# Decoder layer on one core: gate blocks fetched while the last gate blocks are made, and one DRAM tile for each projection and gate block

## The chip, the cores and the metric

The kernel runs on one core of one Trainium2 chip. The metric is the device time of one execution in microseconds, lower is better. Five engines work side by side, each through its own list of instructions in order: TensorE (PE, with PEld for its weight loads), VectorE (DVE), ScalarE (ACT), GpSimd (POOL) and SyncE (SP). In this kernel SP issues the DMAs. An engine waits for another only through semaphores.

## The reference

One layer of a hybrid decoder on 1024 prompt tokens and 32 sample tokens that share their weights, all in fp32:

```python
h = layer_norm(ALPHA * x + 0.5 * swiglu(x, f1_w1, f1_w3, f1_w2), ln1_g, ln1_b)
z = h @ w_in + b_in
...
att = combine_groups(outs, lses).astype(h.dtype)
yb, vrows = sgu_branch(uv, sgu_ln_g, sgu_ln_b, sgu_ws, sgu_b)
mix = (jax.nn.sigmoid(ga) * (att @ w_oa) + jax.nn.sigmoid(gb) * (yb @ w_ob)) @ w_out
h = layer_norm(ALPHA * h + mix, ln2_g, ln2_b)
h = layer_norm(ALPHA * h + 0.5 * swiglu(h, f2_w1, f2_w3, f2_w2), ln3_g, ln3_b)
```

`z` has 5,376 columns: queries, keys and values of three attention groups, the two halves of the gated MLP (SGU), and the gates `ga` and `gb`, 1024 columns each. `combine_groups` weighs the three attention groups by a softmax over their log-sums. `att` has 256 columns, `yb` 512, the model 1024.

## The kernel before, in words

All activations are kept transposed, features on the 128 partitions and the 1056 tokens along the free axis, cut into NC = 4 chunks of C = 264. Every fp32 operand of a large matmul is split into a high and a low part (`split`, L238 on ScalarE and L239 on VectorE), and `mm3` (L227) makes each 128-row product of three matmuls. The 42 column blocks of `z` (128 columns each) are numbered: 0–17 are q, k, v; 18–25 the SGU; 26–33 the blocks of `ga`; 34–41 those of `gb`.

The Tile framework takes the program in the order in which the code names it, sorts each engine's list by a priority that follows that order, and adds the waits. `high_priority(offset=URGENT)` moves what is under it ahead of what the code named shortly before. Tiles come from pools that turn round: 37 slots (`S`, 4.1 KB a partition each), 8 weight tiles (`W`), 2 raw weight tiles (`R`), 6 mid tiles (`M`), 3 PSUM banks for products (`mm_tile`) and 5 for all else (`ax_tile`). An allocation waits until the last user of the tile that it takes over is done. DMAs all go through SP's list, one behind the other, so one that must wait holds all behind it.

**widen** computes `z`. Its first six gate blocks (34 to 39, already with their sigmoid) and all q, k, v and SGU blocks are written to the DRAM scratch `zD`, by `gate8` (L939) and `send` (L1020). `fetch_z` (L1084) brings a whole block of 128 x 1056 back into a slot, with the DMA of L1086.

**mix** makes the last ten gate blocks: six one after the other, then the last four chunk by chunk (the loop over `c` that ends in L1514), each by `gate8`: 24 matmuls into a product bank, a bias on ScalarE into a mid tile (L938), a store to `zD` (L939). `tick` runs, between such steps, pieces of three queues of generators: attention blocks (`attend`, which ends in the store of its statistics L1213), the SGU and `combine` (`mid`), and the sample tokens' attention (`sample`, `sample_join`, L1340 to L1382).

Then follows w_ob. `local(n)` (L1491) is the block n of `yb @ w_ob`: 12 matmuls for each chunk into a product bank, then the product multiply L1489, on VectorE, which multiplies the fetched gate block `mt[n]` (block 34 + n) in place. The first EARLY = 6 run by themselves; then for each n the w_oa product of the same form on `ta[n]` (block 26 + n, 6 matmuls a chunk), with `local(6)` and `local(7)` ahead of n = 0 and 1. Gate blocks made in mix (LATE_GATES: 40, 41 and 26 to 33) get their sigmoid after the fetch, on ScalarE. `mt[n] += ta[n]` (L1564) and a split give the operand of w_out.

Beside the first of these `local` blocks runs `combine(1)`: it loads the attention's minima and sums from DRAM (`mlD`, L1231 to L1237), computes the three groups' weights on 16 partitions (L1245 to L1258), stores them (`cD`, L1260), loads them back spread over 64 partitions each (L1267, six loads of 256 KB), and multiplies and adds the three groups (L1272, L1274, L1275 on 128 x 1024). Its result is split by `split_att` for w_oa. `column_sums` (L1524, L1526) loads blocks of w_out and reduces them in the same stretch.

Of the kernel before, what the change touches and what calls it, by code (L numbers as in the profile page):

```python
# [12 lines left out]
F32 = mybir.dt.float32  # L13
# [7 lines left out]
P = 128  # L21
D = 1024
KB = D // P
NP = 1024
NS = 32
NT = NP + NS
# [28 lines left out]
URGENT = 300  # L55
# [24 lines left out]
class Trunk:  # L80
# [950 lines left out]
    def widen(self):  # L1031
        nc, a = self.nc, self.a
        self.att = [None, None]
        self.attT = {}
        self.mlD = self.dp.tile([2, 3, 2, 2, NP], F32, name="mlD")
        self.cD = self.dp.tile([2, 3, 2, NP], F32, name="cD")
        self.sD = self.dp.tile([3, 3, 4, NS, 64], F32, name="sD")
        self.jD = self.dp.tile([6, 64, 66], F32, name="jD")
        self.zD = self.dp.tile([42, P, NT], F32, name="zD")
        lns, self.lns = self.lns, {}  # L1040
        self.A, Y = self.normed, self.Y
        self.Y = None
        self.T, self.L = ({}, {}), {}
        units, self.early = self.early, None
        preps = {}

        def begin(f):
            preps[f] = self.prep(a["wz7"][f], f, KH * P, nc.gpsimd if f else nc.vector)
            next(preps[f])

        self.drain(lns[NC - 2])
        self.step(self.bg, 1)
        self.slow.append(self.spread(0, Y, self.A, nc.vector))
        for c in range(NC):
            self.drain(lns.pop(c))
            if c == NC - 1:
                self.slow.append(self.spread(1, Y, self.A, nc.vector))
            for n in range(CHUNKED):
                self.gate8(units[n], DENSE[n], c, AF.Sigmoid, STEPS["lead"], 1)
        units = Y = None  # L1060
        for n in range(CHUNKED, NLEAD):
            w = self.unit(a["wzp"][n])
            if n == NLEAD - 1:
                begin(0)
            for c in (1, 3, 0, 2):
                self.gate8(w, DENSE[n], c, AF.Sigmoid, STEPS["lead"], 1)
                if n == NLEAD - 1:
                    next(preps[0], None)
        self.A = None
        for f in range(NZ):  # L1070
            for _ in preps.pop(f):
                pass
            if f < NZ - 1:
                begin(f + 1)

            def between():
                if f + 1 in preps:
                    next(preps[f + 1], None)
                self.tick(STEPS["strassen"], 1)

            self.pair(f, between)
            del self.L[f]
# [389 lines left out]
    def mix(self):  # L1472
        nc, a = self.nc, self.a
        att, mt = [], [None] * KB
# [8 lines left out]
        def product(wo, xs, c, t):  # L1483
            p = self.mm_tile()[:, :C]
            cc = slice(c * C, c * C + C)
            for k, (xh, xl) in enumerate(xs):
                self.mm3(p, wo, k * P, xh[:, cc], xl[:, cc], k == 0, k == len(xs) - 1)
            with self.urgent():
                nc.vector.tensor_tensor(t[:, cc], t[:, cc], p, op=ALU.mult)  # L1489

        def local(n):  # L1491
            wb = self.unit(a["wo"][n, :, 2 * P :], 4 * P)
            if n + 2 < KB:
                mt[n + 2] = self.fetch_z(36 + n)
            if 34 + n in LATE_GATES:
                nc.scalar.activation(mt[n], mt[n], AF.Sigmoid)
            for c in range(NC):
                product(wb, self.yb, c, mt[n])
                self.tick(STEPS["wob"], 1)
# [10 lines left out]
                self.gate8(w, DENSE[n], c, AF.Identity, STEPS["tail"], 1)  # L1510
        units = {n: self.unit(a["wzp"][n]) for n in range(NLEAD + NTAIL - LAST, NLEAD + NTAIL)}
        for c in range(NC):
            for n in units:
                self.gate8(units[n], DENSE[n], c, AF.Identity, STEPS["tail"], 1)  # L1514
        units = self.A = None
        for n in range(2):
            mt[n] = self.fetch_z(34 + n)
        while any(g in self.mid for g in sgu):
            self.step(self.mid, 1)
        def column_sums():  # L1520
# [24 lines left out]
        for n in range(EARLY):  # L1545
            local(n)
# [6 lines left out]
        for n in range(KB):  # L1553
            wa = self.unit(a["wo"][n], 2 * P)
            if n + 2 < KB:
                ta.append(self.fetch_z(28 + n))
            if n < KB - EARLY:
                local(EARLY + n)
            if 26 + n in LATE_GATES:
                nc.scalar.activation(ta[n], ta[n], AF.Sigmoid)  # L1560
            for c in range(NC):
                product(wa, att, c, ta[n])
                self.tick(0, 1)
            nc.vector.tensor_tensor(mt[n], mt[n], ta[n], op=ALU.add)  # L1564
            m2.append((self.S([P, NT], F32R), self.S([P, NT], F32R)))
            self.split(*m2[n], mt[n])
            done += 1
# [204 lines left out]
```

## Time and profile before

| | |
|---|---|
| median of 3 runs | 2226.13 us (2225.06 to 2228.02) |
| the profiled run | 2225.12 us, of which the span that the profile covers is 2223.3 us |
| mean granted TensorE clock | 0.986 |
| busy share of TensorE, VectorE, ScalarE, GpSimd | 97%, 70%, 40%, 15% |
| last store of the last gate blocks | issued 1302.4 us into the span |
| products of w_ob and w_oa | about 1301 to 1406 us into the span |

The profile is one execution, its times are counted from the start of the span. "Busy" is the time in which an engine executes an instruction; "idle before" is what it waited ahead of one, with the instruction that ended the wait (`<-DVE S L1489`: a VectorE instruction of line 1489 that wrote or freed an S tile). In the windows, the granted clock is a share of TensorE's full speed, and the DMA share the mean busy share of the core's 16 DMA engines. The names of tiles stand without their numbers.

### The profile page before, as it was taken

To read this page: it belongs to the slowest core of one execution; us is meant where nothing else is said; L and a number is where in the kernel's file an instruction comes from. 1 tells how busy PE (TensorE), PEld (TensorE's weight loads), DVE (VectorE), ACT (ScalarE), POOL (GpSimd) and SP (SyncE) were. 2 spreads that over 40 slices of the span, in tenths; PEclk is the share of its full clock that TensorE was granted. 3 is DMA by queue.
4 is the path that set the end of the run, shared out by engine and by line. 5 is a ranking of instruction groups with operands and counts; after the bars stand their busy time and mean duration, and the time that the engine had idled before them with its cause. 6 is when DMAs were issued, how large, how long until landed. Compare 5 with 4: busy or idle time off the path is not lost. (4 is left out here: it accounts for less than half of the span.)

```text
span 2223.3 us, 43147 instructions
## 1 busy us (share of the span) xinstructions
PE 2148.0 (97%) x17281; PEld 2095.8 (94%) x17281; DVE 1560.7 (70%) x2698; ACT 898.6 (40%) x1684; POOL 327.1 (15%) x238
## 2 busy tenths in 40 slices
PE   9999999999999999999989969998999999999997
PEld 8999999999999999999879759898999999999997
DVE  8776677656689537787475546778767676657787
ACT  5444444321126533435464533246444444421124
POOL 0433333100000112231000000000422332200000
PEclk9999999999999999999999989999999999999998
DMA  4445445697953336667745455513444545595831
GB/s 156 144 141 186 167 156 184 196 368 266 354 198 131 109 122 208 210 216 247 257 154 174 127 162 193 212 54 116 168 159 165 185 157 179 196 362 218 309 117 79
DMA packets 163640, 416.83 MB, mean 187 GB/s; under 512 B 24096, under 2 KB 60688, under 8 KB 160752
## 3 DMA queue, kind: packets, MB, share of 16 engines
q1 hardware_dynamic: 163008, 413.55, 53.4%
q8 instruction: 135, 2.21, 0.4%
q14 instruction: 65, 0.53, 0.1%
q10 hardware_dynamic: 432, 0.54, 0.1%
HBM read 301.64 MB, written 158.57 MB: 207 GB/s over the span
## 5 line engine op out<-in xcount | busy, mean ns | idle before, releaser
L227 PE MATMUL mm<-S,W 128*128 128x264 f32 x5040 | 677.4, 289 | 43.3 <-DVE S L1489 27.9
L227 PE MATMUL ax<-S,W 128*128 128x264 f32 x5472 | 716.6, 284 | 0.6 <-ACT S L978 0.5
L227 PEld LDWEIGHTS mm<-S,W 128*128 128x128 f32 x5040 | 640.5, 191 | 59.7 <-DVE S L1489 28.1
L227 PEld LDWEIGHTS ax<-S,W 128*128 128x128 f32 x5472 | 685.7, 188 | 3.2 <-ACT S L978 1.9
L227 PE MATMUL ax<-S,S 128*128 128x264 f32 x3288 | 484.7, 284 | 2.2 <-DVE S L987 2.2
L227 PEld LDWEIGHTS ax<-S,S 128*128 128x128 f32 x3288 | 434.5, 188 | 4.3 <-DVE S L987 3.3
L227 PE MATMUL mm<-S,S 128*128 128x264 f32 x2496 | 389.1, 286 | 7.1 <-ACT S L238 4.0
L227 PEld LDWEIGHTS mm<-S,S 128*128 128x128 f32 x2496 | 338.2, 189 | 8.9 <-ACT S L238 4.2
L238 ACT CAST W<-R 128x256 fp32r<-128x256 f32 (+2 forms) x172 | 127.9, 760 | 367.0 <-PE ax L227 134.3
L369 POOL TENSOR_TENSOR Q<-R 128x512 f32<-128x512 f32 x50 | 70.2, 1403 | 792.5 <-DMA R<-w13b 215.9
L239 DVE TENSOR_TENSOR W<-R,W 128x256 fp32r<-128x256 f32 (+2 forms) x172 | 148.4, 870 | 30.4 <-ACT W L238 30.1
L238 ACT CAST W<-Q 128x1024 fp32r<-128x1024 f32 (+1 forms) x79 | 77.8, 984 | 194.9 <-POOL Q L370 90.6
L444 DVE TENSOR_TENSOR S<-ax,M 128x264 f32<-128x264 f32 x84 | 33.4, 433 | 151.7 <-PE ax L227 151.7
L781 DVE SCALAR_TENSOR_TENSOR S<-ax,S 128x264 f32<-128x264 f32 x240 | 99.1, 428 | 56.7 <-PE ax L227 56.2
L239 DVE TENSOR_TENSOR S<-Q,S 128x1024 fp32r<-128x1024 f32 (+2 forms) x87 | 125.7, 1445 | 6.5 <-ACT S L238 5.6
L106 POOL CAST S<-ones 128x1 fp32r<-128x1 f32 x32 | 15.7, 506 | 773.4 <-DVE S L1564 385.4
L238 ACT CAST S<-Q 128x1024 fp32r<-128x1024 f32 (+2 forms) x87 | 86.3, 992 | 100.6 <-PE ax L227 71.7
L239 DVE TENSOR_TENSOR W<-Q,W 128x1024 fp32r<-128x1024 f32 (+1 forms) x79 | 92.3, 1169 | 24.5 <-ACT W L238 24.5
L239 DVE TENSOR_TENSOR S<-S,M 128x528 fp32r<-128x528 f32 x72 | 84.7, 1176 | 3.0 <-ACT M L238 1.3
L370 POOL TENSOR_TENSOR Q<-Q,R 128x512 f32<-128x512 f32 x50 | 84.8, 1696 | 2.7
L238 ACT CAST S<-R 128x512 fp32r<-128x512 f32 (+1 forms) x65 | 44.4, 686 | 94.9 <-DMA sumsA<-S 43.5
L377 POOL TENSOR_TENSOR Q<-R,Q 128x512 f32<-128x512 f32 x50 | 82.2, 1645 | 1.2
(201 smaller groups left out, 2069.6 us busy)
## 6 DMA issues: line engine op xcount, KB each, us to landing
ws<-st SPq DMA_DIRECT2D x144, 256.0 KB
S<-sumsA SPq DMA_DIRECT2D x63, 528.0 KB
S<-sumsB SPq DMA_DIRECT2D x63, 528.0 KB
M<-kv SPq DMA_DIRECT2D x96, 256.0 KB
sumsA<-M SPq DMA_DIRECT2D x90, 264.0 KB
sumsB<-M SPq DMA_DIRECT2D x90, 264.0 KB
R<-w13b SPq DMA_DIRECT2D x44, 512.0 KB
S<-zD SPq DMA_DIRECT2D x42, 528.0 KB
```

What stands on the lines that cost most here:

```text
L106: self.nc.gpsimd.tensor_copy(t[:, 0, :1] if len(shape) == 3 else t[:, :1], self.ones[:, :1])
L227: mm = lambda a, b, s, e: nc.tensor.matmul(o, a[:, cc], b, start=s, stop=e, skip_group_check=True)
L238: a = self.nc.scalar.copy(hi, src)
L239: b = self.nc.vector.tensor_tensor(lo, src, hi.bitcast(F32), op=ALU.subtract)
L369: tt(s12[:, lo], cd[:, lo], cd[:, hi], op=ALU.add)
L370: tt(s12[:, hi], s12[:, lo], ab[:, lo], op=ALU.subtract)
L377: tt(s34[:, hi], ab[:, hi], s12[:, hi], op=ALU.subtract)
L444: go(one, 5, False, lambda x: tt(h[:, x, 1], one[x], p7[:, x], op=ALU.add))
L781: nc.vector.scalar_tensor_tensor(y(x, r, e), bank[x], HALF, y(x, r, e), op0=ALU.mult, op1=ALU.add)
```

## The change

The scratch `zD` becomes a list of 42 DRAM tiles, one a block, where it was one tile. The fetches of blocks 34 to 39 move from behind the gate loops (two) and from `local(0)` to `local(3)` (four) into the loop of the last gate blocks: two each ahead of chunks 1, 2 and 3, under high priority. `local(0)` and `local(1)` now fetch blocks 40 and 41, under high priority too. Lines from 1494 on move down, by one behind the fetch of `local`, by three behind the gate loop.

```diff
--- before.py
+++ after.py
@@ -1036,7 +1036,7 @@
         self.cD = self.dp.tile([2, 3, 2, NP], F32, name="cD")
         self.sD = self.dp.tile([3, 3, 4, NS, 64], F32, name="sD")
         self.jD = self.dp.tile([6, 64, 66], F32, name="jD")
-        self.zD = self.dp.tile([42, P, NT], F32, name="zD")
+        self.zD = [self.dp.tile([P, NT], F32, name=f"zD{n}") for n in range(42)]
         lns, self.lns = self.lns, {}
         self.A, Y = self.normed, self.Y
         self.Y = None
@@ -1490,8 +1490,9 @@
 
         def local(n):
             wb = self.unit(a["wo"][n, :, 2 * P :], 4 * P)
-            if n + 2 < KB:
-                mt[n + 2] = self.fetch_z(36 + n)
+            if n + 6 < KB:
+                with self.tc.high_priority(offset=URGENT):
+                    mt[n + 6] = self.fetch_z(40 + n)
             if 34 + n in LATE_GATES:
                 nc.scalar.activation(mt[n], mt[n], AF.Sigmoid)
             for c in range(NC):
@@ -1510,11 +1511,13 @@
                 self.gate8(w, DENSE[n], c, AF.Identity, STEPS["tail"], 1)
         units = {n: self.unit(a["wzp"][n]) for n in range(NLEAD + NTAIL - LAST, NLEAD + NTAIL)}
         for c in range(NC):
+            if c:
+                with self.tc.high_priority(offset=URGENT):
+                    for n in range(2 * c - 2, 2 * c):
+                        mt[n] = self.fetch_z(34 + n)
             for n in units:
                 self.gate8(units[n], DENSE[n], c, AF.Identity, STEPS["tail"], 1)
         units = self.A = None
-        for n in range(2):
-            mt[n] = self.fetch_z(34 + n)
         while any(g in self.mid for g in sgu):
             self.step(self.mid, 1)
         def column_sums():
```

SP's list in the last gate blocks, before. `zD` is the scratch, `M` a mid tile of one chunk, `R` a raw weight tile, `ws` and `st` an output and an input that are copied through:

```order
L939 DMA zD<-M_14929 128x264
L939 DMA zD<-M_14986 128x264
L939 DMA zD<-M_15077 128x264
L939 DMA zD<-M_15124 128x264
L1213 DMA mlD<-X_14827 32x128
L939 DMA zD<-M_15167 128x264
L217 DMA R_15479<-wo 128x512
L210 DMA ws<-st 16x4096
L939 DMA zD<-M_15242 128x264
L217 DMA R_15544<-wo 128x512
```

and with the change, where the gate blocks' tiles are numbered (`zD_8611` is block 34, `zD_8607` block 30):

```order
L939 DMA zD_8607<-M_14978 128x264
L939 DMA zD_8608<-M_15035 128x264
L1086 DMA S_14714<-zD_8611 128x1056
L1086 DMA S_14716<-zD_8612 128x1056
L939 DMA zD_8609<-M_15126 128x264
L939 DMA zD_8610<-M_15173 128x264
L1213 DMA mlD<-X_14872 32x128
L939 DMA zD_8607<-M_15220 128x264
L217 DMA R_15528<-wo 128x512
L210 DMA ws<-st 16x4096
L1086 DMA S_14949<-zD_8613 128x1056
L1086 DMA S_14951<-zD_8614 128x1056
```

Four of the six fetches stand there now, among the stores of the gate blocks.

SP's list around combine's weights, before, from the loads of `mlD` on:

```order
L1237 DMA S_15175<-mlD 8x16x8 x4
L1524 DMA Q_15685<-wout 128x1024
L1260 DMA cD<-S_15175 16x128 x3
L1267 DMA S_15208<-cD 64x1024 x2
L1267 DMA S_15209<-cD 64x1024 x2
L1267 DMA S_15210<-cD 64x1024 x2
L1086 DMA S_15320<-zD 128x1056
L1086 DMA S_15322<-zD 128x1056
L1086 DMA S_15331<-zD 128x1056
L1086 DMA S_15408<-zD 128x1056
L1086 DMA S_15486<-zD 128x1056
```

and with the change:

```order
L1237 DMA S_15228<-mlD 8x16x8 x4
L217 DMA R_15809<-wo 128x256
L1360 DMA M_15415<-jD 64x66 x2
L1527 DMA Q_15728<-wout 128x1024
L210 DMA ws<-st 16x4096 x2
L217 DMA R_15818<-wo 128x512
L210 DMA ws<-st 16x4096
L1260 DMA cD<-S_15228 16x128 x3
L1267 DMA S_15261<-cD 64x1024 x2
L1267 DMA S_15262<-cD 64x1024 x2
L1267 DMA S_15263<-cD 64x1024
L1086 DMA S_15380<-zD_8617 128x1056
```

The fetches of blocks 34 to 39 no longer follow the `cD` loads; two weight loads, the sample's `jD` load and three state copies have moved ahead of the `cD` stores. Blocks 40 and 41 (the first of them is the last row) are fetched between the two halves of the third `cD` load.

VectorE's list at the first product multiplies, before. `S_15320` is the block 34:

```order
L1256 RECIPROCAL X_15188<-X_15188 16x128
L1258 TENSOR_TENSOR S_15175<-X_15188,S_15175 16x128 x3
L1272 TENSOR_TENSOR S_15207<-S_14166,S_15208 128x1024
L1274 TENSOR_TENSOR S_14560<-S_14560,S_15209 128x1024
L1275 TENSOR_TENSOR S_15207<-S_15207,S_14560 128x1024
L1274 TENSOR_TENSOR S_14883<-S_14883,S_15210 128x1024
L1489 TENSOR_TENSOR S_15320<-S_15320,mm_15333 128x264
L1489 TENSOR_TENSOR S_15320<-S_15320,mm_15351 128x264
L1489 TENSOR_TENSOR S_15320<-S_15320,mm_15373 128x264
```

and with the change, where block 34 is `S_14714`:

```order
L239 TENSOR_TENSOR W_15593<-R_15591,W_15592 128x512
L1489 TENSOR_TENSOR S_14714<-S_14714,mm_15382 128x264
L1340 TENSOR_TENSOR M_13116<-M_13116,X_13020 128x64x4
L1345 TENSOR_REDUCE X_15397<-M_13116 128x64
L1346 TENSOR_TENSOR X_13023<-X_13023,X_15397 128x64
L1489 TENSOR_TENSOR S_14714<-S_14714,mm_15400 128x264
L1211 COPY X_15183<-ax_15181 32x128
L1489 TENSOR_TENSOR S_14714<-S_14714,mm_15422 128x264
L1489 TENSOR_TENSOR S_14714<-S_14714,mm_15436 128x264
L239 TENSOR_TENSOR W_15666<-R_15664,W_15665 128x512
L1245 COPY X_15241<-S_15228 16x128
L1489 TENSOR_TENSOR S_14716<-S_14716,mm_15459 128x264
```

The first multiply stood behind the whole of combine; it now stands ahead of all of it, and combine's small operations (L1245 and on) stand between the multiplies of block 35.

VectorE's list where combine's weights are used, with the change. `S_14951` is block 37, `S_15260` the combined attention:

```order
L1373 SCALAR_TENSOR_TENSOR X_15523<-M_15415,X_15515,X_15523 128x64
L1376 COPY X_15523<-X_15523 128x64
L1489 TENSOR_TENSOR S_14951<-S_14951,mm_15598 128x264
L1489 TENSOR_TENSOR S_14951<-S_14951,mm_15612 128x264
L1272 TENSOR_TENSOR S_15260<-S_14207,S_15261 128x1024
L1382 COPY S_14155<-ax_15626 64x32 x2
L1382 COPY S_15260<-ax_15626 64x32 x2
L1489 TENSOR_TENSOR S_14951<-S_14951,mm_15636 128x264
L1274 TENSOR_TENSOR S_14601<-S_14601,S_15262 128x1024
L1489 TENSOR_TENSOR S_14951<-S_14951,mm_15650 128x264
L239 TENSOR_TENSOR W_15820<-R_15818,W_15819 128x512
L1275 TENSOR_TENSOR S_15260<-S_15260,S_14601 128x1024
```

L1272, which needs the first `cD` load, stands behind two multiplies of block 37, and its third multiply stands behind L1272.

## The prediction

> **What bounds the kernel now.** I read the page first: TensorE is busy 97% of the span, so only time in which it stands still, or runs at a lower clock, can be won.
>
> ```profile
> PE 2148.0 (97%) x17281; PEld 2095.8 (94%) x17281; DVE 1560.7 (70%) x2698; ACT 898.6 (40%) x1684; POOL 327.1 (15%) x238
> L227 PE MATMUL mm<-S,W 128*128 128x264 f32 x5040 | 677.4, 289 | 43.3 <-DVE S L1489 27.9
> ```
>
> The second row is the group of all matmuls into the three product banks. The waits of TensorE (total, times, longest):
>
> ```profile
> PE mm L227 <- DVE S L1489: 27.9, 9, 20.9
> PE mm L227 <- ACT M L938: 6.3, 3, 2.9
> ```
>
> One stands out: 20.9 of the 27.9 us that matmuls wait for the product multiply of L1489 are a single stall. The timelines around it show why, TensorE's first, then VectorE's, then that of SP, which issues the DMAs.
>
> ```profile
> 1306.75 0.66 PE L1187 MATMUL ax<-S,Q 128*64 128x128 f32 x8
> 1328.29 24.53 PE L227 MATMUL mm<-S,W 128*128 128x264 f32 x189 [20.88 <-DVE S L1489]
> 1352.69 27.56 PE L227 MATMUL mm<-S,W 128*128 128x264 f32 x225
> ```
>
> ```profile
> 1315.45 0.87 DVE L1258 TENSOR_TENSOR S<-X,S 16x128 f32<-16x128 f32 x3
> 1321.89 1.23 DVE L1272 TENSOR_TENSOR S<-S,S 128x1024 f32<-128x1024 f32 x1 [5.58 <-DMA S<-cD]
> 1324.11 1.22 DVE L1274 TENSOR_TENSOR S<-S,S 128x1024 f32<-128x1024 f32 x1 [0.99 <-DMA S<-cD]
> 1325.37 1.23 DVE L1275 TENSOR_TENSOR S<-S,S 128x1024 f32<-128x1024 f32 x1
> 1326.67 1.23 DVE L1274 TENSOR_TENSOR S<-S,S 128x1024 f32<-128x1024 f32 x1
> 1327.81 1.10 DVE L1489 TENSOR_TENSOR S<-S,mm 128x264 f32<-128x264 f32 x3
> ```
>
> ```profile
> 1315.76 1.24 SPq L1260 DMA_DIRECT2D cD<-S  x3
> 1317.14 3.65 SPq L1267 DMA_DIRECT2D S<-cD  x6
> 1320.84 9.73 SPq L1086 DMA_DIRECT2D S<-zD  x11
> ```
>
> TensorE stops at 1306.75 + 0.66 = 1307.41: w_ob's first three chunk products fill its three banks. What frees them, the multiplies at 1327.81, stands on VectorE behind the whole of combine: small operations up to L1258, the weights' way to DRAM and back (L1260, L1267), four 128x1024 operations. The gate operand itself is fetched only from 1320.84, behind combine's loads. So two causes stand in series: the late fetch, and the place in VectorE's order that follows from it.
>
> The windows (length, busy by engine with counts for PE, PEld, DVE, ACT and POOL, then granted clock, DMA share, GB/s) price the rest.
>
> ```profile
> 1260.00:1280.00 20.00, 20.00 (x147) 15.05 (x148) 5.41 (x28) 10.90 (x36) 0.00 (x0) 1.00 0.06 22
> 1307.40:1328.30 20.90, 0.02 (x2) 0.01 (x1) 10.43 (x20) 2.47 (x3) 0.00 (x0) 0.58 0.58 161
> 1320.00:1340.00 20.00, 11.71 (x85) 11.71 (x86) 13.60 (x21) 5.10 (x6) 0.00 (x0) 0.72 1.02 352
> 1328.30:1366.20 37.90, 37.90 (x301) 37.90 (x302) 23.01 (x55) 12.41 (x17) 0.00 (x0) 0.96 0.61 213
> 1377.80:1406.00 28.20, 20.37 (x146) 18.12 (x145) 26.22 (x45) 14.12 (x16) 0.00 (x0) 1.00 0.60 210
> ```
>
> **What the change removes.** The first multiply now stands ahead of combine's operations, and its operand is requested in the gate stage. The 20.88 us go. The clock does too: 0.58 in the stall and 0.96 after it. At full clock a matmul takes 27.56/225 = 0.1225 us; the 189 that follow the stall would take 23.15 and took 24.53, so 1.4 us more are removable. Together 22.3 us.
>
> **What the early fetches cost.** Eight fetches move, 528 KB each; none is added. By 352 GB/s in 1320–1340 one takes about 1.5 us. Blocks 34 and 35 now stand on SP between the second and third of four gate stores that run from 1254.62, blocks 36 and 37 behind two weight and state loads some 20 us later, and 38 and 39 ahead of combine's mlD traffic.
>
> ```profile
> 1254.62 22.14 SPq L939 DMA_DIRECT2D zD<-M  x4
> 1302.42 0.38 SPq L939 DMA_DIRECT2D zD<-M  x1
> ```
>
> ```profile
> 1245.01 1.37 PE L227 MATMUL mm<-S,W 128*128 128x264 f32 x9
> 1254.15 0.66 PE L1128 MATMUL ax<-ident,S 128*128 128x128 f32 x4
> ```
>
> In 1260–1280 the DMA engines are 0.06 busy, so the transfers are free there. A fetch needs a free slot, and everything behind it on SP (gate stores, weight loads, mlD loads) waits if none is free. By the built program the slots that these six take are released by TensorE instructions of 1245–1255, which the last two rows bracket, before SP reaches the fetches (about 1260 for the first two, some way into the four stores). I take 0; if that cover goes, it is the third rival. The separate DRAM tiles add no instruction: 0.
>
> **What VectorE must do instead.** Between TensorE's stop and the first w_oa product lie 25 chunk products of 12 matmuls (the rest of block 0, blocks 1 to 5, and block 6 which precedes w_oa's first): 300 x 0.1225 = 36.7 us. VectorE's work for the same stretch is 10.43 + 23.01 = 33.4 us. It fits, but hardly, and it is in order with one wait inside. I walk through it. Rows: a multiply and the other steps cost
>
> ```profile
> L1489 DVE TENSOR_TENSOR S<-S,mm 128x264 f32<-128x264 f32 x64 | 25.9, 426 | 13.5 <-PE mm L227 13.2
> L1526 DVE TENSOR_REDUCE X<-Q 128x8 f32<-128x1024 f32 x5 | 6.1, 1212 | 0.0
> L239 DVE TENSOR_TENSOR W<-R,W 128x512 fp32r<-128x512 f32 x5 | 3.4, 690 | 1.9 <-ACT W L238 1.7
> L239 DVE TENSOR_TENSOR S<-S,S 128x1024 fp32r<-128x1024 f32 x2 | 2.4, 1218 | 0.0
> L239 DVE TENSOR_TENSOR W<-R,W 128x256 fp32r<-128x256 f32 x8 | 3.4, 421 | 1.0 <-ACT W L238 1.0
> ```
>
> One chunk product takes 1.47 us. In the new order L1258 stands behind the multiply of block 2's third chunk (counting from 0), whose matmuls end eight chunks after 1307.41, at 1319.2. With 0.43 for the multiply and 0.87 for L1258: 1320.5, where it was 1316.3. From L1258's end to L1272's start it took 1321.89 - 1316.32 = 5.57 us, so L1272 starts at 1326.1, VectorE having idled some 2 us for it. Behind L1272 stands the multiply of block 3's third chunk, ready since 1325.0. TensorE has its three banks in hand, until 1328.0; the multiply ends at 1326.1 + 1.23 + about 0.5 (L1382) + 0.43 = 1328.3. First stall: 0.3. After that nearly every multiply has a 1.2 us operation ahead of it: behind L1274 0.2; behind a 0.69 split and L1275 0.85; behind att's split (1.22) 0.3; behind the second L1274 0.2; behind a row reduction, a split and the last L1275 (1.21 + 0.42 + 1.23) 0.8. Then VectorE catches up, at about 1341. Sum of the stalls: 2.65, I take 2.7 us.
>
> Bounds: below, 0, if combine's weights come back soon enough that VectorE never falls behind three banks. Above, 2.7 + 3.5 + 1.4 = 7.6: cD's loads now stand behind two more weight loads and two to three state copies of 256 KB, so they may land up to about 3.5 us later (four or five such pieces at half a fetch, 0.75 us, each), and one stall would then be long enough to lower the clock again, at the 1.4 of before. The nearest row, cD's own 5.57 us in an otherwise quiet queue, speaks for the lower half. The second half of the third cD load stands behind two fetches, 3.0 us; it is needed by the second L1274 at about 1334, and its old landing (before 1326.67) moved by 4.2 + 3.0 falls there too, so 0 to 1 us, in the range. The Trainium skill, "DMA: Bandwidth & Descriptors", Queues, rings and completion order, says that on each DMA engine descriptors are consumed in ring order: by it the half load does pay the two fetches; without such an order it would pay nothing, and the sum the same within 1 us.
>
> **Later.** From 1377.8 VectorE bounds: 26.22 of 28.2 us. The order there is the same, so this stage shifts as a whole and neither gives nor takes.
>
> **The sum.** 22.3 - 2.7 = 19.6 us. Span 2223.3 - 19.6 = 2203.7. The profiled run took 2225.12, 1.8 around its span: 2205.5. The median of the runs, 2226.13, is 1.0 above it: **2206.5 us**.
>
> **Rivals.**
> A. VectorE lags more: cD's loads come late and the stalls are longer, 6 to 13 us instead of 2.7. For it: 33.4 of 36.7 us leave little slack, and combine's four loads and adds, att's splits and the row reductions all lie in one stretch. Against: TensorE has three banks of cover each time. Gain 9 to 16: 2210 to 2217. From 1382 to 1404 gaps of up to 2.43 us leave the clock at 1.00, while the 20.88 us gap brought 0.58:
>
> ```profile
> 1381.98 2.41 PE L227 MATMUL mm<-S,W 128*128 128x264 f32 x18 [0.59 <-DVE S L1489]
> 1400.61 2.45 PE L227 MATMUL mm<-S,W 128*128 128x264 f32 x18 [2.43 <-DVE S L1489]
> ```
>
> The Trainium skill, "TensorE: Matmul & The Clock Gate", Part 1, puts the limit at an idle window of about 3.4 us; both rows agree with it. By it none of my six stalls lowers the clock, and only this rival pays 1.4 us for it.
>
> B. Nothing is given back: 2226.13 - 22.3 = 2203.8. VectorE would have to be earlier than its order lets it.
>
> C. Slower: the fetches hold SP. If a slot were freed only when the last attention block ends, at about 1306, SP would stand from 1260 until then. Gate stores would not go out, so the six mid buffers and then the banks fill. A gate chunk is 24 matmuls, 2.9 us; three banks and two free buffers cover 14.7 us, all six 26.4. The loss is 46 less this cover, 20 to 31 us, against the gain of 19.6: about 2226 to 2238. With the smaller cover it decides when the slot is freed after 1260 + 14.7 + 19.6 = 1294. Against it are the releases at 1245–1255. The end of the last attention block, its copy on VectorE:
>
> ```profile
> 1305.88 0.28 DVE L1211 COPY X<-ax 32x128 f32<-32x128 f32 x1 [3.91 <-PE ax L1209]
> ```
>
> D. No effect: the first multiply still waits, as its operand or its place is still behind combine: 2226. Against it is the order of the built program, where it stands first.
>
> **Chances.** Forecast (2204.2 to 2209.5) 0.67; A 0.18; B 0.06; C 0.06; D 0.03. The range takes in the forecast, B and most of A: 2202.5 to 2214, about 0.85 of the chance. A measurement tells 0.2%, 4.5 us, from no change; A, B and the forecast lie beyond it: faster 0.91, within 0.03, slower 0.06.
>
> **What would show it.** In the changed kernel the 20.9 us wait should be gone, the longest wait of a product matmul for the multiply between 1300 and 1345 under 2 us and their sum 2 to 4, and the granted clock there 1.0. L1272 should start at about 1326 after a wait for cD, and w_oa's first product follow at about 1307.4 + 36.7 + 2.7 = 1347, instead of 1366 (1352.69 plus the other 111 of the 300 matmuls). The gate stage up to 1307 should keep its times within 0.5 us; matmuls or sigmoids waiting there on stores would be rival C. A single stall over 3.4 us with a clock below 1.0 would be rival A.

## The result, and the profile after

| | before | changed |
|---|---|---|
| median | 2226.04 us (2225.06 to 2228.02, 4 runs) | 2207.45 us (2206.12 to 2210.04, 4 runs) |
| the profiled run, its span | 2225.12, 2223.3 us | 2207.8, 2206.0 us |

The ratio of the runs is 0.9917, with a 95% interval of 0.9900 to 0.9934: 18.6 us less. The forecast was 2206.5 us.

TensorE's busy time on the page of the changed kernel, and its waits:

```profile
PE 2153.6 (98%) x17281; PEld 2101.2 (95%) x17281; DVE 1558.2 (71%) x2698; ACT 895.4 (41%) x1682; POOL 327.1 (15%) x238
```

```profile
PE mm L227 <- DVE S L1489: 9.5, 10, 2.4
PE mm L227 <- ACT S L238: 5.1, 3, 3.3
```

The waits for the product multiply fell from 27.9 to 9.5 us and none is longer than 2.4. The place itself, in TensorE's timeline of the changed kernel (start, duration, instruction, count, idle before and its releaser):

```profile
1306.23 16.01 PE L227 MATMUL mm<-S,W 128*128 128x264 f32 x130
1322.08 0.27 PE L1379 MATMUL ax<-ident,X 128*128 128x128 f32 x1
1322.10 3.42 PE L227 MATMUL mm<-S,W 128*128 128x264 f32 x26
1327.26 1.72 PE L227 MATMUL mm<-S,W 128*128 128x264 f32 x12 [1.74 <-DVE S L1489]
1329.93 1.70 PE L227 MATMUL mm<-S,W 128*128 128x264 f32 x12 [0.95 <-DVE S L1489]
1332.01 3.37 PE L227 MATMUL mm<-S,W 128*128 128x264 f32 x24 [0.38 <-DVE S L1489]
1335.80 25.59 PE L227 MATMUL mm<-S,W 128*128 128x264 f32 x204 [0.41 <-DVE S L1489]
```

One stall of 20.88 us became four, 3.48 us together. VectorE's timeline shows what each hangs on:

```profile
1299.71 0.43 DVE L1489 TENSOR_TENSOR S<-S,mm 128x264 f32<-128x264 f32 x1 [0.66 <-PE mm L227]
...
1308.13 0.22 DVE L1245 COPY X<-S 16x128 f32<-16x128 f32 x1 [1.14 <-DMA S<-mlD]
...
1317.04 0.90 DVE L1258 TENSOR_TENSOR S<-X,S 16x128 f32<-16x128 f32 x3
...
1324.79 1.23 DVE L1272 TENSOR_TENSOR S<-S,S 128x1024 f32<-128x1024 f32 x1 [3.27 <-DMA S<-cD]
...
1328.31 1.23 DVE L1274 TENSOR_TENSOR S<-S,S 128x1024 f32<-128x1024 f32 x1 [1.11 <-DMA S<-cD]
...
1334.17 1.23 DVE L1274 TENSOR_TENSOR S<-S,S 128x1024 f32<-128x1024 f32 x1 [0.64 <-DMA S<-cD]
```

The first multiply now runs 8.4 us ahead of combine's first operation and waits for nothing but its matmuls. The three waits for combine's weights (3.27, 1.11 and 0.64 us) each stand ahead of a multiply that TensorE needs. In the windows of the changed kernel (columns as in the prediction) the clock is whole:

```profile
1300.00:1320.00 20.00, 20.00 (x168) 19.05 (x167) 14.14 (x43) 4.18 (x8) 0.00 (x0) 1.00 0.56 170
1320.00:1340.00 20.00, 16.40 (x125) 15.21 (x124) 13.84 (x27) 8.98 (x11) 0.00 (x0) 1.00 0.86 257
```

**A measure that holds still.** The total scatters by several us from run to run (more on that at the end), so I measure the part in which the change acts between two instructions that every version has: the last attention block's transposition on TensorE (L1209) and the first sum of the two branches on VectorE (L1564, now L1567). Before, then changed:

```profile
1305.57 0.27 PE L1209 MATMUL ax<-ident,X 128*32 128x128 f32 x1
...
1371.12 1.25 DVE L1564 TENSOR_TENSOR S<-S,S 128x1056 f32<-128x1056 f32 x1
```

```profile
1302.66 0.27 PE L1209 MATMUL ax<-ident,X 128*32 128x128 f32 x1
...
1351.37 1.25 DVE L1567 TENSOR_TENSOR S<-S,S 128x1056 f32<-128x1056 f32 x1
```

That is 65.55 and 48.71 us: the part is 16.8 us shorter. The rest of the 17.3 us between the two spans is what lies around it: 2.9 us less ahead of L1209, 0.7 less from the first sum to the last, 3.2 more from there to the end. Neither the 2.9 nor the 3.2 is shown to come from the change: the kernel before, profiled again (e10), has L1209 at 1302.02, earlier still. The first and the last sum of the changed kernel stand in its row of the eight (shortest, median and longest duration, first and last start):

```profile
L1567 DVE TENSOR_TENSOR S<-S,S x8: 1249/1251/1259, 1351.4 to 1387.3; 128x1056 f32<-128x1056 f32 x8
```

### The profile page after: what moved, and what is told of

Read it like the earlier page. It is cut to its first block, busy times and chain, and to the rows that moved or that the text cites. A ratio compares the mean times of both kernels' runs of the same rounds, so it can differ in the third digit from the quotient of the medians.

```text
span 2206.0 us, 43143 instructions
## 1 busy us (share of the span) xinstructions
PE 2153.6 (98%) x17281; PEld 2101.2 (95%) x17281; DVE 1558.2 (71%) x2698; ACT 895.4 (41%) x1682; POOL 327.1 (15%) x238
## 4 chain that ended last, share of the span: by engine, by line
PE 84%; DVE 5%; DMA 5%; issue 2%; ACT 1%; POOL 1%; SPq 0%; ACTq 0%; DVEq 0%; POOLq 0%
PE ax L227 43%; PE mm L227 36%; DMA M<-kv 2%; PE ax L1148 1%; DVE S L239 1%; DMA R<-wz 1%; PE ax L1171 1%; PE ax L1187 1%; DVE W L239 1%; DVE X L1330 1%; DMA S<-zD 0%; DMA S<-cD 0%; DVE M L1329 0%; DVE S L605 0%; POOL Q L370 0%
```

## The experiments

"The part" is this stretch; the spans of single profiles are not compared. A table first:

| version | the part, us | stalls of w_ob's matmuls behind L1489, us | median, us | ratio to before, 95% interval |
|---|---|---|---|---|
| before; again (e10) | 65.55; 66.77 | 20.9; 21.0 | 2226.04; 2223.92 (one run) | |
| changed; again (e11) | 48.71; 47.78 | 3.5; 2.8 | 2207.45; 2207.84 | 0.9900–0.9934; 0.9907–0.9937 |
| e1, one DRAM tile | 48.60 | 3.6 | 2208.19 | 0.9913–0.9942 |
| e2, two early fetches | 61.38 | 13.3 | 2223.24 | 0.9972–0.9999 |
| e3, no wait for cD | 46.63 | 2.1 | 2206.66 | 0.9902–0.9936 |
| e4, no copies | 47.56 | 2.7 | 2208.52 | 0.9907–0.9949 |
| e5, 40 and 41 late | 48.93 | 3.4 | 2209.88 | 0.9915–0.9945 |
| e6, e4 and e5 | 47.39 | 3.3 | 2209.90 | 0.9917–0.9945 |
| e7, e3 and e5 | 45.66 | 1.5 | 2203.81 (one run) | |
| e8, six at chunk 0; again (e12) | 46.49; 45.55 | 1.7; 0.8 | 2206.14; 2205.62 | 0.9896–0.9934; 0.9901–0.9931 |
| e9, e4 and e8 | 45.28 | 0.9 | 2208.90 | 0.9905–0.9936 |

In e3 and e7 the profile puts 0.69 and 1.52 us of these stalls down to L1364, a small reduction of the sample's attention. In the built program the matmul waits for the semaphore value of the multiply L1489 just ahead of it on VectorE, so these stalls are counted here.

**Does the measure repeat?** The kernel before, once more:

> The kernel before once more, for a second profile. Theory (w_ob's part repeats, what lies around it does not): from the last attention block's transposition to the first sum 65.5 us within 0.5, one stall of 20.9 us; the stretches at half clock elsewhere lie at other places than in the first profile, the time up to w_ob differs by 1 to 5 us. Rival (the profile of before was typical in all parts, and the changed kernel's later stretches at half clock near 1500 are its own): the same stretches as in the first profile, none between 1490 and 1530.

```profile
1302.02 0.27 PE L1209 MATMUL ax<-ident,X 128*32 128x128 f32 x1
...
1324.84 25.65 PE L227 MATMUL mm<-S,W 128*128 128x264 f32 x189 [20.99 <-DVE S L1489]
```

The stall is the same, 20.99 us. The part is 66.77 us (the first sum starts at 1368.79), 1.2 more, and the 189 matmuls behind the stall took 25.65 us instead of 24.53: the lowered clock lasted longer. L1209 starts 3.5 us earlier than in the first profile. So the part repeats within about 1.2 us, less well than expected, but far better than what lies around it.

**Which half of the change acts.**

```diff
-        self.zD = [self.dp.tile([P, NT], F32, name=f"zD{n}") for n in range(42)]
+        self.zD = self.dp.tile([42, P, NT], F32, name="zD")
```

> The change with the scratch as one DRAM tile again: only the place of the fetches differs from the kernel before. Theory (the place of the fetches pays, the separate tiles do nothing): 2207 us within 2, the 20.9 us stall absent, stalls of w_ob's matmuls 3 to 4 us in all. Rival (the separate tiles pay, as a fetch from one tile waits for the gate stores ahead of it): SP stands at the fetches until the stores have landed, and the time is 2212 to 2226.

The part took 48.60 us, within 0.1 of the changed kernel, at a median of 2208.19. The built instruction lists of all engines, with their waits, are the same with one tile and with 42, for the changed kernel and for the kernel before; so the kernel before with 42 tiles was not run. The separate tiles do nothing; the place of the fetches does all. The priority in the gate loop does nothing either: without it the lists are the same (not run).

**Is the first operand enough?** Only blocks 34 and 35 early, in the last gate chunk:

```diff
-            if c:
+            if c == NC - 1:
                 with self.tc.high_priority(offset=URGENT):
-                    for n in range(2 * c - 2, 2 * c):
+                    for n in range(2):
                         mt[n] = self.fetch_z(34 + n)
...
-            if n + 6 < KB:
-                with self.tc.high_priority(offset=URGENT):
-                    mt[n + 6] = self.fetch_z(40 + n)
+            if n + 2 < KB:
+                mt[n + 2] = self.fetch_z(36 + n)
```

> Only blocks 34 and 35 are fetched in the last gate chunk, the other six as in the kernel before. Theory (the place of the multiplies in VectorE's order pays): TensorE does blocks 0 and 1 and three chunks of block 2, eleven chunk products, then waits behind combine from about 1316 to 1327: one stall of 10 to 12 us, and 1.4 for a lowered clock after it; gain 8 to 11, time 2215 to 2218. Rival (what was missing was the first operand alone; once VectorE has begun, the rest follows): 2207 to 2209, no stall over 2 us.

TensorE and VectorE of this kernel:

```profile
1304.73 13.43 PE L227 MATMUL mm<-S,W 128*128 128x264 f32 x96 [1.99 <-DVE S L1489]
...
1330.14 41.99 PE L227 MATMUL mm<-S,W 128*128 128x264 f32 x324 [11.29 <-DVE S L1489]
```

```profile
1304.24 1.11 DVE L1489 TENSOR_TENSOR S<-S,mm 128x264 f32<-128x264 f32 x3 [2.76 <-DMA S<-zD]
...
1323.42 1.23 DVE L1272 TENSOR_TENSOR S<-S,S 128x1024 f32<-128x1024 f32 x1 [3.73 <-DMA S<-cD]
```

The stall behind combine is 11.29 us, as expected: block 2 now waits where block 0 waited before. The time was not: 2223.24, against 2215 to 2218. I had left out that a fetch in the last chunk lands late (2.76 us of wait, 1.99 of it on TensorE) and that the clock falls twice: behind the first stall 96 matmuls take 13.43 us where 0.1225 each would give 11.8, behind the second 324 take 41.99 where it would give 39.7. The part is 4 to 5 us shorter than before, not 8 to 11. The median is only 2.1 us below that of the kernel before in the same series, 2225.37; the ten runs scatter over 13 us. So the gain needs the operand of every block whose multiply would otherwise stand behind combine, and time for it to land.

**What gives back some of the gain.** First, combine without its round trip; it then uses the weights of the first pair of heads, and the second pair's are left out:

```diff
-                nc.sync.dma_start(cb[64 * h : 64 * h + 64], self.cD[hp, g, h].partition_broadcast(64))
+                nc.sync.dma_start(cb[64 * h : 64 * h + 64], self.cD[0, g, h].partition_broadcast(64))
```

> combine of the second pair of heads loads the weights of the first pair, which lie in DRAM long before, so nothing waits for the cD round trip (the second pair's weights are left out of the result). Theory (the 3.5 us of stalls left come from the wait for cD): stalls of w_ob's matmuls 0 to 1 us in all, time 2204 to 2205.5. Rival (they come from VectorE's load, 33.4 us of work in 36.7): 2.5 to 3.5 us remain, time 2207.

The part was 46.63, 1 to 2 us less; the largest stall left, 1.21 us, stands behind two splits and the last L1275, VectorE's work without a wait. The next, 0.69, stands behind the second L1274, which still waited 1.08 us for its half load behind two fetches. The stalls sum to 2.1, between the two theories, and the median is near the second. One caution: the edit also moves L1272 and the first L1274 forward in VectorE's list, ahead of L1256, so it changes the order along with the wait. The state copies, held back from the weights of w_ob and the first two w_oa blocks:

```diff
+            held, self.copies = self.copies, []
             wb = self.unit(a["wo"][n, :, 2 * P :], 4 * P)
+            self.copies = held
...
+            held, self.copies = self.copies, self.copies if n > 1 else []
             wa = self.unit(a["wo"][n], 2 * P)
+            self.copies = held
```

> No state copies are issued with the weights of w_ob and of the first two w_oa blocks; they are issued later. Theory (SP reaches the cD loads late because its DMA semaphores are held by the copies ahead): the loads follow the cD stores within 0.2 us instead of 1.3, L1272 starts 1 to 1.5 us earlier, stalls 2 to 2.5 us instead of 3.5, time about 2206. Rival (the way of cD through DRAM itself is slow): L1272 as before and stalls 3.5, time 2207.5.

SP's timeline of the changed kernel, then of this one:

```profile
1317.34 1.27 SPq L1260 DMA_DIRECT2D cD<-S  x3
1319.94 3.05 SPq L1267 DMA_DIRECT2D S<-cD  x5
1323.04 1.05 SPq L1086 DMA_DIRECT2D S<-zD  x2
1324.13 0.51 SPq L1267 DMA_DIRECT2D S<-cD  x1
```

```profile
1322.92 1.26 SPq L1260 DMA_DIRECT2D cD<-S  x3
1324.31 3.01 SPq L1267 DMA_DIRECT2D S<-cD  x5
```

SP's wait ahead of the cD loads, 1.33 us in the changed kernel, is 0.13 here, and the first stall 0.59 instead of 1.74. But the changed kernel's second profile (e11) shows the loads 0.15 us behind the stores with the copies in place, and a first stall of 0.41. Over all versions whose loads wait for these stores, the wait is 0.13 us in the three profiles without the copies (e4, e6, e9) and 0.14 to 1.33 in the seven with early fetches and copies. So with the copies the loads are late in some executions, not in all. The way that I had supposed is not what the profile shows: it puts SP's 1.3 us down to the first cD store, which had not yet landed, and not to a copy. The difference of the parts, 0.2 to 1.2 us, is no more than the scatter of that part. The edit also reorders TensorE's list in the gate stage, so more than the copies differs. Then the fetches of blocks 40 and 41, behind the cD loads:

```diff
             if n + 6 < KB:
-                with self.tc.high_priority(offset=URGENT):
-                    mt[n + 6] = self.fetch_z(40 + n)
+                mt[n + 6] = self.fetch_z(40 + n)
```

> The changed kernel with the fetches of blocks 40 and 41 without priority: they stand behind the third cD load on SP instead of between its halves (VectorE's second L1274 then stands one multiply earlier). Theory (the half load pays for the two fetches ahead of it): the second L1274 no longer waits for cD, the stall of 0.4 to 1.9 us behind it goes, stalls of w_ob's matmuls 2 to 3 us in all, time 0.5 to 1.5 us below the changed kernel. Rival (VectorE's load alone sets the stalls): the stall moves to the next multiply and the sum stays at 3.5.

A miss. The sum of the stalls stayed at 3.4, the part at 48.93. The second L1274 still waited, 1.28 us, as it now stood two multiplies earlier on VectorE, ahead of the first L1275, and one stall grew to 2.84; the clock was 0.66 in the 5 us behind it. Both together:

> Both: no state copies ahead of the cD stores, and blocks 40 and 41 behind the cD loads. Theory (both delays of cD cost on their own): cD loads 0.1 us behind the stores, L1272 6.6 us after L1258's start, no wait before the second L1274, stalls 1 to 2 us in all; time 1.5 to 2.5 below the changed kernel, about 2205. Rival (VectorE's load): 3 us or more remain.

The part is 47.39, the stalls 3.3, no better than the copies alone. The expected 1 to 2 us did not come, for the same reason.

> As the run without the wait for cD (the first pair's weights in place of the second's), and blocks 40 and 41 behind the cD loads: nothing of combine waits for a round trip or a fetch. What is left is VectorE's own load. Theory: under 1 us of stalls. Rival: 2 us, as without the moved fetches.

With the round trip and the half load both out of the way, the part is 45.66, and one stall of w_ob's matmuls is left, on TensorE and with what VectorE did ahead of it:

```profile
1325.34 13.48 PE L227 MATMUL mm<-S,W 128*128 128x264 f32 x107 [1.52 <-DVE X L1364]
```

```profile
1321.17 0.41 DVE L1489 TENSOR_TENSOR S<-S,mm 128x264 f32<-128x264 f32 x1
1321.78 1.23 DVE L1274 TENSOR_TENSOR S<-S,S 128x1024 f32<-128x1024 f32 x1 [0.21 <-DMA S<-cD]
1322.92 1.22 DVE L1275 TENSOR_TENSOR S<-S,S 128x1024 f32<-128x1024 f32 x1
1324.06 0.93 DVE L1256 RECIPROCAL X<-X 16x128 f32<-16x128 f32 x1
1324.92 0.36 DVE L1489 TENSOR_TENSOR S<-S,mm 128x264 f32<-128x264 f32 x1
```

The matmul starts 0.06 us behind the end of the last multiply shown, whose bank it takes. Between that multiply and the one before it VectorE worked through three operations of combine and idled 0.21 us. So this stall is VectorE's own load: it costs about 1.5 us in this order, between the two theories. The changed kernel's 2.8 to 3.6 us were that and the waits for combine's weights, together; how they divide depends on the order.

**Do early fetches hold SP?** All six ahead of the first of the last gate chunks:

```diff
-            if c:
+            if c == 0:
                 with self.tc.high_priority(offset=URGENT):
-                    for n in range(2 * c - 2, 2 * c):
+                    for n in range(EARLY):
                         mt[n] = self.fetch_z(34 + n)
```

> All six fetches ahead of chunk 0 of the last gate blocks, on SP ahead of the fetches of the last attention block's q, k and v and behind slots that are released from about 1226 to 1240. Theory (SP is held only until those slots are free and the six transfers cost 1.5 us each): the last attention block's operands land up to 9 us later, which gate matmuls hide; stalls before 1300 grow by 0 to 3 us, w_ob as in the changed kernel, time 2207 to 2211. The prediction's third rival (fetches that hold SP stop the gate stores and so TensorE): a stall of 5 us or more on the mid tiles or on the zD loads in the gate stage, time over 2212.

TensorE kept its one wait in the gate stage, for a mid tile (0.9 us between 1215 and 1300, as in the changed kernel), and the part got shorter by about 2 us, which I had not expected. Run once more beside the changed kernel:

> The changed kernel once more, beside the next one on the same chip. Theory: the part from the last attention block's transposition to the first sum 48.7 us within 0.4; time 2207 to 2209. Rival (that part too is scatter): it differs by more than 1 us from 48.7.

> The six fetches ahead of chunk 0 once more. Theory (mlD's loads start earlier without two fetches ahead of them, so combine does): the same part 46.5 us within 0.4, and the median 1 to 3 us below the changed kernel's of the same call. Rival (the gain of the part is given back elsewhere, or the scatter hides it): medians within 1 us.

SP at the start of combine in these two runs, the changed kernel first:

```profile
1303.07 0.90 SPq L1086 DMA_DIRECT2D S<-zD  x2
1304.38 0.32 SPq L1213 DMA_DIRECT2D mlD<-X  x1
1304.75 1.33 SPq L1231 DMA_DIRECT2D S<-mlD  x4
1306.13 3.17 SPq L1233 DMA_DIRECT2D S<-mlD  x4
```

```profile
1303.32 0.66 SPq L1231 DMA_DIRECT2D S<-mlD  x2
1304.63 0.31 SPq L1213 DMA_DIRECT2D mlD<-X  x1
1304.98 0.65 SPq L1231 DMA_DIRECT2D S<-mlD  x2
1305.68 1.33 SPq L1233 DMA_DIRECT2D S<-mlD  x4
```

Without two fetches of 528 KB ahead of them, the twelve small loads of mlD go out in about 1.33 us a group; behind the fetches the second group takes 3.17, of which SP waits 2.0 for the fetches to land. In the nine profiles of versions with the two fetches there that wait is 1.7 to 2.3 us, in the other five it is absent. It is a wait that the program sets: in the built list SP's DMAs take eight semaphores in turn, and the second group's second and third loads use those of the two fetches, so they are held until these have landed. L1258 starts 13.0 us after L1209 instead of 14.4, and TensorE's stalls fall from 2.8 to 0.8. The parts are 47.78 and 45.55, against 48.71 and 46.49 in the earlier runs: both 0.9 below what was expected of a repeat, and each time 2.2 us apart. Half of it is lost again at once: from the first sum to the last it is 37.1 us with the six fetches at chunk 0, both times, against 35.9 and 36.1 of the changed kernel, so 1.0 and 1.1 us are left up to the last sum. Why stays open: the granted clock over that stage is 0.95 in e12, but 0.95 in the first profile of the changed kernel as well. The medians, 2207.84 and 2205.62, lie 2.2 apart, but their intervals overlap: shorter in its part is shown, faster in total is not.

> All six fetches ahead of chunk 0, and no state copies with the weights of w_ob and the first two w_oa blocks. Theory (the way of combine's weights is what the rest of the loss hangs on: without fetches ahead of the mlD loads it starts 1.3 us earlier, without copies the cD loads follow their stores at once): from the last attention block's transposition to the first sum of w_ob and w_oa 45 to 46.5 us, where the changed kernel took 48.7; stalls of w_ob's matmuls 0.5 to 1.5 us; time 2 to 3 us below the changed kernel, about 2205. Rival (VectorE's load): 47 us or more, time as with the six fetches alone, 2206.

The part is the shortest of all versions that compute the reference, 45.28, the stalls 0.9. The median is 2208.90, not the 2205 expected. All three versions without the copies were no faster than the changed kernel although their part was shorter. From the last sum to the end their profiles take 818.3 to 819.7 us, the other eleven 814.4 to 819.4, so the copies may cost something where they went; two of the eleven lie as high, and this stays open.

## Why the prediction was right

By its own steps:

- **What bounds, and what the change removes.** Right. The stall of 20.88 us is gone, the first multiply stands ahead of combine, and the clock after it is 1.00 where it was 0.96. By the second profile of before (189 matmuls in 25.65 us, 2.5 us over full speed) up to 23.5 us were removable, not 22.3.
- **Early fetches at no cost.** Right for the gate stage, and the third rival (SP held) fell twice: in the changed kernel, and with all six fetches ahead of chunk 0, the last pair some 50 us earlier still. It was not quite free behind it: the last pair held the mlD loads, as the repeat of the six fetches showed. The sign that the gate stage keeps its times within 0.5 us was too strict, for L1209 moved by 3.5 us between two profiles of the kernel before.
- **What VectorE must do instead.** The mechanism was right, the size was not. The walk through VectorE's order had L1258 end 14.9 us after the L1209 of its time base and it ended 15.3 after it. The stalls were to sum to 2.7; they sum to 3.5, 3.6 and 2.8 in three profiles of this program. Two things were mis-sized. The wait for cD, 5.57 us from L1258's end to L1272, was 6.85 in the first profile: SP reached the loads 1.3 us late. In e11 it was 5.5, and there the stalls sum to 2.8, as forecast. And a stall costs more than its gap: the 12 matmuls behind the first and the second take 1.72 and 1.70 us, in a run 1.47, and the 24 and the 204 behind the other two lost 0.4 and 0.6 against 0.1225 a matmul, 1.5 us in all. The gaps and this make 5.0 of the 22.3 - 16.8 = 5.5 us that were given back in this pair of profiles, where 2.7 was forecast; it is inside the bounds, 0 to 7.6.
- **The sum.** The term given back was half of what it measured. Mean of the part before 66.2 (two profiles), changed 48.4 (three of this program): 17.8 us, and 0.7 from a shorter w_oa stage, against 19.6 forecast. That agrees with the 18.6 between the medians. That the total came within 1 us is partly luck: some 2.4 us more were given back than forecast, and the larger removable loss of the second profile (0.6 in the mean) and the w_oa stage (0.7, forecast as nothing) made up for half of it.
- **Later.** Nearly right: from the first sum to the last it is 36.6 before and 35.9 after, where no difference was forecast. From there to the end the changed kernel's profile is 3.2 us longer, but the twelve other profiles spread over 5 us there, so no cause is claimed.
- **The rivals.** A (6 to 13 us given back) was not reached, but 5.5 lies nearer to it than to 2.7. B fell with the four stalls. D fell with the first row of VectorE's timeline. The sentence under A that none of the stalls lowers the clock came true, at a clock of 1.00 in the windows and a longest stall of 1.74 us, but by luck: in e2 and e5 stalls of 1.99 and 2.84 us were followed by a lowered clock, and the last section has more.

## What to carry to other kernels

An operand that is fetched late can cost far more than its transfer: here its consumer had been put behind other work in VectorE's list, and as VectorE took its list in order, TensorE waited for that work as well. Look at what stands in the consumer's list ahead of the waiting instruction before pricing the fetch, and fetch every operand whose consumer would stand there, not the first alone. When the wait is gone, look next at the small loads that a chain of operations hangs on, and at the semaphores that they share with bulk transfers: here two bulk fetches out of the way of twelve loads of 4 KB made the part 2.2 us shorter, though half of that was lost again in the next stage. And check who really releases a wait: the profile names the instruction that signalled last, which twice was not the one waited for.

## What the runs showed of the hardware

The granted clock fell after far shorter gaps than the prediction allowed for. At one place ahead of the change, where the program is the same, 14 matmuls follow a gap of about 1 us. In the changed kernel and in e3:

```profile
1226.26 1.97 PE L227 MATMUL mm<-S,W 128*128 128x264 f32 x14 [0.91 <-ACT M L938]
```

```profile
1227.92 3.45 PE L227 MATMUL mm<-S,W 128*128 128x264 f32 x14 [1.04 <-ACT M L938]
```

```profile
1227.00:1237.00 10.00, 9.08 (x43) 7.91 (x43) 8.82 (x19) 4.78 (x14) 0.00 (x0) 0.51 0.26 94
```

In e3 the clock stayed at 0.51 for 10 us; its matmuls lie 1.5 us behind the changed kernel's before this stretch and 5.9 behind it, so it cost some 4.3 us. In the changed kernel the clock did not fall there. In e12 it did, behind a gap only 0.01 us longer than the changed kernel's:

```profile
1226.25 3.37 PE L227 MATMUL mm<-S,W 128*128 128x264 f32 x14 [0.92 <-ACT M L938]
```

Two executions of the kernel before show it at another place, behind gaps of 2.03 and 2.01 us:

```profile
1516.84 2.81 PE L227 MATMUL mm<-S,S 128*128 128x264 f32 x21 [2.03 <-ACT M L415]
```

```profile
1514.58 4.35 PE L227 MATMUL mm<-S,S 128*128 128x264 f32 x21 [2.01 <-ACT M L415]
```

The length of the last gap alone does not decide. The sentence of the prediction on the Trainium skill ("TensorE: Matmul & The Clock Gate", Part 1), that the limit is an idle window of about 3.4 us, does not hold for these rows: the clock fell behind gaps of 0.92, 1.04 and 2.01 us. Such stretches come and go between executions of one program and move its total by several us: L1209 started between 1300.9 and 1308.5 us in profiles whose program is the same up to the last gate blocks (those without the copies left aside). That is why the part, and not the total, told the versions apart.
